# Two reload sets fetched two tiles ahead, and three PSUM tiles that swap banks, in a one-core fp32 layer

## The chip, the cores and the metric

The kernel runs on one core of one Trainium2 chip. The metric is the time of one execution on the device, in microseconds, and the median of several runs is compared. A core has TensorE (PE in the profile, with its weight loads as PEld), VectorE (DVE), ScalarE (ACT), GpSimd (POOL) and SyncE (SP), which here issues nearly all DMAs. Each engine works through its own instructions in the order in which the program put them; an instruction that waits holds everything behind it on that engine. That holds for SP's DMA issues too.

## What is computed

One layer of a decoder trunk for 1024 tokens of 2048 features, all in fp32:

```python
h = rmsnorm(x, g_pre)
u = h @ w_in                       # columns: gq gk gv g_gate g_lr | sq sk sv s_gate
log_a = log_sigmoid(g_lr @ w_a2 + b_a) / 16
o_gla = rmsnorm(gla_chunked(gq, gk, gv, log_a), g_gla_head) * silu(g_gate)   # 4 heads
o_sb  = stick_breaking(sq, sk, sv) * silu(s_gate)                            # 8 heads of 128
mix = concat(o_gla, o_sb) @ w_out
x = x + rmsnorm(mix, g_post)
gate = sigmoid(x @ w_ple_gate + b_ple_gate)
out = x + gate * (p @ w_ple_proj)
```

## The kernel before

Every fp32 operand of a large product is split into a high part, rounded by ScalarE (`hi`, `ah`, `wh`), and a low part, the rest, subtracted by VectorE (`lo`, `al`, `wl`). A product of two such operands takes three matmuls (line 101): high by high, low weight by high activation, high weight by low activation. The tokens are handled in two halves of 512 columns, `hf` 0 and 1.

The input projection goes by units of 128 columns of `w_in`. The first two units run beside the loading of x and fill all four PSUM buffers of the tag `dn` (`first`, evacuated by ScalarE in line 736). From the third unit on `dense` is called: it takes two PSUM tiles of the tag `dn`, and its weights come through `wload`: a DMA into one of two `raw` buffers, a split into one of four `hi` and `lo` buffers each. PSUM has eight banks: four `dn`, two `z`, one `t`, one `o`. The small work of the two attention parts uses `z`, `t` and `o`.

After the second unit two jobs per half are queued as urgent: `norm_first` (the sum of squares of x over all features through a matmul with ones in `rsqrt_mean`, then 1/sqrt of the mean as `rstd`) and `low_rank` (the forget gate's 16 columns, through a matmul with a selection matrix; `W3` steps pass between its split and its matmuls). The evacuation of the third unit and of all later ones multiplies by `rstd`, and the heads' jobs (`gla`, then `sb`) start when no urgent job is left. The jobs are generators; `step()`, called within the dense products, advances one or more of them. `beside` is a third queue of background jobs, of which one piece is taken every `pace[1]` steps. A scheduler then orders the instructions of each engine by its own estimates.

After the last unit comes C11: the eight products of one quarter of the gate weights `w_gate[0, 0]` (`keep_u1`), then eight with `w_gate[1, 0]` (`keep_11`, the last four after the attention's buffers were given back). Beside them the last head's attention ends, and `x_set` brings back two sums of x that were stored to DRAM earlier: the set `S2` beside the first eight products, the set `S1` beside the next four. A set has eight tiles of 128 by 512: each is loaded by a DMA into a buffer of the tag `u` (twelve buffers, shared with the attention) and split into `ah` and `al`. What is not done when the fourth of the `keep_11` products ends is done in a loop without products.

Then the gate stage starts. Its loop over j loads three quarters of the gate weights (`wr`, four buffers of 512 KB, line 880), subtracts twice on VectorE (line 876), splits the results into `wh` and `wl`, and runs two products with `S2` and `S1`. The `wr` buffers lie where the attention's buffers were. A loop that the text calls T4 follows, with the sum of one quarter and a stored difference as weights.

## Time and profile before

| | |
|---|---|
| time, median of 3 runs | 2092.18 us (2090.54 to 2094.57) |
| the profiled execution: its own time | 2090.99 us |
| the profiled execution: its span, first to last instruction | 2089.3 us |
| granted clock of TensorE, mean, as a share of full speed | 0.997 |
| TensorE busy | 2068.5 us, 99% of the span, 9712 matmuls |
| VectorE busy | 1483.5 us, 71% |
| ScalarE busy | 875.1 us, 42% |
| DMA, mean over the span | 169 GB/s |

A matmul of 512 columns is listed with a duration of about 0.39 us, but consecutive ones start about 0.23 us apart: they overlap, and their listed ends are modelled. So the pace of TensorE is read from the starts, and a wait as a start that comes late. The share of 99% is one of overlapping durations; time in which TensorE runs at half its clock counts as busy.

### The profile page before, as it was taken

To read this page: it belongs to the slowest core of one execution; us is meant where nothing else is said; L and a number is where in the kernel's file an instruction comes from. 1 tells how busy PE (TensorE), PEld (TensorE's weight loads), DVE (VectorE), ACT (ScalarE), POOL (GpSimd) and SP (SyncE) were. 2 spreads that over 40 slices of the span, in tenths; PEclk is the share of its full clock that TensorE was granted. 3 is DMA by queue.
4 is the path that set the end of the run, shared out by engine and by line. 5 is a ranking of instruction groups with operands and counts; after the bars stand their busy time and mean duration, and the time that the engine had idled before them with its cause. 6 is when DMAs were issued, how large, how long until landed. Compare 5 with 4: busy or idle time off the path is not lost.

```text
span 2089.3 us, 26740 instructions
## 1 busy us (share of the span) xinstructions
PE 2068.5 (99%) x9712; PEld 1709.3 (82%) x9712; DVE 1483.5 (71%) x2243; ACT 875.1 (42%) x1390; POOL 108.1 (5%) x229
## 2 busy tenths in 40 slices
PE   9999999999999999999999899999999999999998
PEld 6788888888888888888888788888788888788887
DVE  8657777676776676666567667788777687886765
ACT  7333334333464455555456413344233434323332
POOL 4100000000011111101101000000000000000000
PEclk9999999999999999999999999999999999999999
DMA  6222222232344344433335677988977586886763
GB/s 217 69 71 72 86 73 86 66 86 66 76 112 99 102 108 111 110 94 100 80 89 161 207 291 275 324 302 295 328 282 260 183 321 219 295 279 211 238 206 105
DMA packets 229700, 352.81 MB, mean 169 GB/s; under 512 B 124336, under 2 KB 129344, under 8 KB 229568
## 3 DMA queue, kind: packets, MB, share of 16 engines
q1 hardware_dynamic: 228960, 349.00, 52.7%
q10 hardware_dynamic: 576, 2.10, 0.3%
q8 instruction: 76, 1.25, 0.3%
q14 instruction: 56, 0.46, 0.1%
q0 software_dynamic: 32, 0.01, 0.0%
HBM read 249.85 MB, written 73.92 MB: 155 GB/s over the span
## 4 chain that ended last, share of the span: by engine, by line
PE 73%; DMA 10%; DVE 9%; issue 5%; ACT 2%; SPq 1%; POOL 0%; DVEq 0%; ACTq 0%; POOLq 0%
PE dn L101 63%; PE z L101 5%; DMA E<-X 3%; PE o L101 2%; PE t L101 2%; DVE wl L114 1%; DMA wr<-w_out 1%; DMA u<-S1x_d 1%; DVE X L603 1%; DMA ar<-og_d 1%; DVE lo L114 1%; DVE al L114 1%; DMA h_d<-st 1%; DMA ar<-h_d 1%; DVE rstd L235 0%
## 5 line engine op out<-in xcount | busy, mean ns | idle before, releaser
L101 PE MATMUL dn<-ah,hi 128*128 128x512 f32 x1408 | 562.6, 400 | 2.0 <-ACT u L736 1.6
L101 PE MATMUL dn<-ah,lo 128*128 128x512 f32 x1408 | 550.2, 391 | 0.7 <-DVE lo L114 0.7
L101 PE MATMUL dn<-al,hi 128*128 128x512 f32 x1408 | 550.1, 391 | 0.1
L101 PE MATMUL dn<-ah,wl 128*128 128x512 f32 x1216 | 474.9, 391 | 1.6 <-DVE wl L114 1.5
L101 PE MATMUL dn<-ah,wh 128*128 128x512 f32 x1216 | 474.2, 390 | 1.8 <-ACT wh L113 1.8
L101 PE MATMUL dn<-al,wh 128*128 128x512 f32 x1216 | 474.3, 390 | 0.0
L101 PEld LDWEIGHTS dn<-ah,hi 128*128 128x128 f32 x1408 | 265.4, 188 | 60.2 <-issue 3.6
L101 PEld LDWEIGHTS dn<-al,hi 128*128 128x128 f32 x1408 | 264.6, 188 | 57.8 <-DVE al L252 0.5
L101 PEld LDWEIGHTS dn<-ah,lo 128*128 128x128 f32 x1408 | 265.6, 189 | 49.0 <-DVE lo L114 1.3
L113 ACT ACTIVATE wh<-wr 128x1024 fp32r<-128x1024 f32 x152 | 159.1, 1056 | 307.2 <-DVE wr L876 148.5
L101 PEld LDWEIGHTS dn<-ah,wl 128*128 128x128 f32 x1216 | 228.9, 188 | 50.9 <-DVE wl L114 3.3
L101 PEld LDWEIGHTS dn<-ah,wh 128*128 128x128 f32 x1216 | 229.0, 188 | 49.9 <-ACT wh L113 2.5
L101 PEld LDWEIGHTS dn<-al,wh 128*128 128x128 f32 x1216 | 229.0, 188 | 47.7
L114 DVE TENSOR_TENSOR wl<-wr,wh 128x1024 fp32r<-128x1024 f32 x152 | 184.9, 1217 | 6.3 <-ACT wh L113 6.2
L113 ACT ACTIVATE hi<-raw 128x512 fp32r<-128x512 f32 x192 | 119.8, 626 | 147.7 <-PE dn L101 138.5
L114 DVE TENSOR_TENSOR lo<-raw,hi 128x512 fp32r<-128x512 f32 x192 | 135.3, 706 | 52.4 <-ACT hi L113 52.1
L333 ACT ACTIVATE X<-E 128x256 uint16<-128x256 uint16 (+2 forms) x96 | 81.0, 844 | 139.2 <-DMA E<-X 72.0
L876 DVE TENSOR_TENSOR wr<-wr,wr 128x1024 f32<-128x1024 f32 x48 | 58.7, 1224 | 72.0 <-issue 20.0
L603 DVE TENSOR_TENSOR_SCAN X<-X 128x128 f32<-128x128 f32 (+2 forms) x96 | 97.9, 1020 | 14.5 <-POOL X L597 13.1
L618 DVE COPY v<-E 128x512 uint16<-128x512 uint16 (+1 forms) x160 | 64.5, 430 | 48.4 <-DMA E<-X 45.2
L114 DVE TENSOR_TENSOR s<-v,s 128x512 fp32r<-128x512 f32 (+1 forms) x82 | 52.6, 641 | 63.2 <-ACT s L113 62.8
L873 DVE TENSOR_TENSOR wr<-wr,wr 128x1024 f32<-128x1024 f32 x48 | 58.7, 1224 | 43.8 <-DMA wr<-w_g 26.5
(246 smaller groups left out, 2288.7 us busy)
## 6 DMA issues: line engine op xcount, KB each, us to landing
raw<-w_in SPq DMA_DIRECT2D x160, 256.0 KB, 2.7
wr<-w_g SPq DMA_DIRECT2D x64, 512.0 KB, 4.3
wr<-w_out SPq DMA_DIRECT2D x56, 512.0 KB, 4.9
wr<-w_gate SPq DMA_DIRECT2D x40, 512.0 KB, 5.6
g_d<-wr SPq DMA_DIRECT2D x32, 512.0 KB, 2.6
wr<-g_d SPq DMA_DIRECT2D x32, 512.0 KB, 5.1
ar<-h_d SPq DMA_DIRECT2D x28, 512.0 KB, 5.2
ar<-og_d SPq DMA_DIRECT2D x25, 512.0 KB, 5.4
```

Of the source, the lines that this page charges most:

```text
L101: PE.matmul(o, lhsT, rhs, start=start, stop=stop)
L113: A.activation(hi, src, AF.Copy)
L114: (eng or V).tensor_tensor(lo, src, f(hi), op=ALU.subtract)
L333: A.activation(pl.rearrange("p (two n) -> p two n", two=2), src.bitcast(U16)[:, :2 * n].rearrange("p (n two) -> p two n", two=2), AF.Copy)
L603: V.tensor_tensor_scan(rev, rev, rev, initial=kq[:, n:n + 1], op0=ALU.mult, op1=ALU.bypass)
L618: V.tensor_copy(to[:, :, :m, j], w[:, :, 2 * g:2 * g + m])
L873: V.tensor_tensor(dst, a, b, op=ALU.add)
L876: V.tensor_tensor(dst, a, b, op=ALU.subtract)
```

## The change

Four things are edited.

1. The third unit (`u == 2`) accumulates in two `z` banks, not `dn`; the two sums of `norm_first` (`rsqrt_mean` called from there) go to `dn`, not `z`.
2. `W3` is 9, not 4: `low_rank` lets nine steps pass, not four, between its split and its matmuls.
3. `x_set` loads two tiles before its first pause, and then in each piece splits the tile loaded longest ago and loads the one two further on. Before, a piece loaded one tile, and the next piece split it.
4. For the set `S1` a background piece is taken every 2 steps, not every 4 (`pace[1] = 2`).

```diff
-W3 = 4
+W3 = 9
...
-    def dense(wsrc, acts, halves, evac):
-        out_ps = {hf: ps("dn") for hf in halves}
+    def dense(wsrc, acts, halves, evac, bank="dn"):
+        out_ps = {hf: ps(bank) for hf in halves}
...
-    def rsqrt_mean(acc, n, dst, new):
-        z = ps("z")
+    def rsqrt_mean(acc, n, dst, new, bank="z"):
+        z = ps(bank)
...
-            rsqrt_mean(acc[hf], D, acc[hf], lambda dt=F32: at(next(tags), dt=dt))
+            rsqrt_mean(acc[hf], D, acc[hf], lambda dt=F32: at(next(tags), dt=dt), "dn")
...
-                dense(U(u), x_act, HALVES, ev)
+                dense(U(u), x_act, HALVES, ev, "z" if u == 2 else "dn")
...
         def x_set(name, hf):
-            for k in range(8):
+            def load(k):
                 t = at("u")
                 dma2(t, part(sx_d[name][k // 2], k))
-                yield 1
+                return t
+
+            ahead_2 = [load(0), load(1)]
+            yield 1
+            for k in range(8):
                 if k % 2 == 0:
                     wides = act_wide(hf, k // 2)
                 pair = tuple(part(x, k) for x in wides)
-                split(*pair, t)
+                split(*pair, ahead_2.pop(0))
                 g_sets[name].append(pair)
+                if k + 2 < 8:
+                    ahead_2.append(load(k + 2))
+                yield 1
...
         beside.append(x_set("S1", 0))
+        pace[1] = 2
```

Three places show what this does to the order. The first is on TensorE, where the third unit starts. Before (names with numbers: `dn_727` and `dn_728` are the unit's two halves):

```order
L268 MATMUL o_80<-xraw_590,lr_w 32x512
L101 MATMUL dn_727<-ah_123,hi_730 128x512
L101 MATMUL dn_727<-ah_123,lo_731 128x512
L101 MATMUL dn_727<-al_124,hi_730 128x512
L101 MATMUL dn_728<-ah_135,hi_730 128x512
```

And now:

```order
L268 MATMUL o_80<-xraw_590,lr_w 32x512
L101 MATMUL z_727<-ah_123,hi_730 128x512
L101 MATMUL z_727<-ah_123,lo_731 128x512
L101 MATMUL z_727<-al_124,hi_730 128x512
L101 MATMUL z_728<-ah_135,hi_730 128x512
```

The order is the same, the banks are others. Where that unit ends, VectorE had this order (`v<-t` and `v<-o` are the first step of `low_rank` for the two halves, `v<-dn_727` is the third unit's evacuation):

```order
L677 TENSOR_TENSOR v_845<-t_79,rstd_259 128x512
L114 TENSOR_TENSOR s_847<-v_845,s_846 128x512
L677 TENSOR_TENSOR v_886<-o_80,rstd_271 128x512
L685 TENSOR_TENSOR lr_690<-z_881,lr_690 32x512
L114 TENSOR_TENSOR s_888<-v_886,s_887 128x512
L323 TENSOR_TENSOR v_904<-dn_727,rstd_259 128x512
```

And now:

```order
L677 TENSOR_TENSOR v_845<-t_79,rstd_259 128x512
L114 TENSOR_TENSOR s_847<-v_845,s_846 128x512
L323 TENSOR_TENSOR v_893<-z_727,rstd_259 128x512
L323 TENSOR_TENSOR v_896<-z_728,rstd_271 128x512
L685 TENSOR_TENSOR lr_690<-z_925,lr_690 32x512
```

Both evacuations moved ahead of `low_rank`'s result for the first half, and its second half moved behind them. On TensorE the first half's selection matmuls stand 19 matmuls into the fourth unit, where they stood 13 into it, and the heads' first gate matmul (`z<-lr,a2c`) stands 24 dense matmuls later. From the third head's gla work on, TensorE's order is the same again as before.

The second place is ScalarE in C11, where the last head's attention and the set S1 meet. Before:

```order
L333 ACTIVATE X_2345_11059<-E_2344_11053 128x1024
L113 ACTIVATE s_11078<-v_11075 128x512
L113 ACTIVATE ah_11205<-u_11137 128x512
L113 ACTIVATE hi_11240<-raw_11239 128x512
L113 ACTIVATE s_11115<-v_11112 128x384
L113 ACTIVATE ah_11205<-u_11209 128x512
```

And now:

```order
L333 ACTIVATE X_2346_11061<-E_2345_11055 128x1024
L113 ACTIVATE s_11078<-v_11075 128x512
L113 ACTIVATE ah_11141<-u_11106 128x512
L113 ACTIVATE ah_11141<-u_11108 128x512
L113 ACTIVATE hi_11256<-raw_11255 128x512
L113 ACTIVATE s_11119<-v_11116 128x384
```

Two tiles of S1 are split where one was. The last split of S2 (`ah_11069<-u_11073`) stood 10 rows ahead of `s_11078` and now stands 46 rows ahead of it. The last split of S1 had two splits of `raw` weights behind it before the next stage, and now has six.

The third place is SP's queue at the end of C11. Before:

```order
L763 DMA u_11338<-S1x_d_706 128x512
L763 DMA u_11344<-S1x_d_706 128x512
L130 DMA raw_11473<-w_gate 128x512
L130 DMA raw_11491<-w_gate 128x512
L880 DMA wr_11596<-w_gate 128x1024
L880 DMA wr_11598<-w_gate 128x1024
L880 DMA wr_11600<-w_gate 128x1024
L880 DMA wr_11667<-w_gate 128x1024
```

And now (line 888 is the former line 880):

```order
L130 DMA raw_11451<-w_gate 128x512
L888 DMA wr_11596<-w_gate 128x1024
L130 DMA raw_11473<-w_gate 128x512
L888 DMA wr_11598<-w_gate 128x1024
L130 DMA raw_11491<-w_gate 128x512
L888 DMA wr_11600<-w_gate 128x1024
L888 DMA wr_11667<-w_gate 128x1024
```

The loads of S1 are done ahead of this piece, and the first two of the next stage's four loads moved ahead of the last `raw` loads of C11.

## Rows read from the trace of the kernel before

**Rows 1.** The page, busy time of each engine (us, share, instructions)

```profile
PE 2068.5 (99%) x9712; PEld 1709.3 (82%) x9712; DVE 1483.5 (71%) x2243; ACT 875.1 (42%) x1390; POOL 108.1 (5%) x229
```

**Rows 2.** Timeline of TensorE: start, duration, line, tiles, count [idle before <-releaser]

```profile
57.72 1.07 PE L268 MATMUL t<-xraw,lr_w 128*32 128x512 f32 x8
58.71 0.50 PE L101 MATMUL dn<-ah,hi 128*128 128x512 f32 x1
...
60.30 1.07 PE L268 MATMUL o<-xraw,lr_w 128*32 128x512 f32 x8
62.94 0.50 PE L101 MATMUL dn<-ah,hi 128*128 128x512 f32 x1 [1.57 <-ACT u L736]
```

**Rows 3.** Busy time by stretch: PE, PEld, DVE, ACT, POOL (count), PEclk, DMA share, GB/s

```profile
60.00:64.00 4.00, 2.43 (x15) 1.05 (x14) 1.39 (x2) 2.87 (x6) 0.00 (x0) 1.00 0.47 128
1150.00:1165.00 15.00, 12.21 (x50) 8.80 (x49) 9.46 (x16) 8.20 (x14) 0.00 (x0) 0.89 0.69 157
...
1197.00:1210.00 13.00, 10.40 (x32) 7.76 (x31) 9.98 (x10) 3.60 (x4) 0.00 (x0) 0.74 0.72 258
1285.00:1335.00 50.00, 50.00 (x222) 41.23 (x221) 40.68 (x40) 22.34 (x22) 0.00 (x0) 1.00 0.91 317
```

**Rows 4.** Chain of work, first units: start us, us, what

```profile
77.81 11.11 PE dn L101 x49
...
92.67 7.50 PE dn L101 x33
```

**Rows 5.** Timeline of VectorE after the third unit

```profile
88.77 0.69 DVE L114 TENSOR_TENSOR s<-v,s 128x512 fp32r<-128x512 f32 x1 [0.70 <-ACT s L113]
...
92.12 0.69 DVE L323 TENSOR_TENSOR v<-dn,rstd 128x512 f32<-128x512 f32 x1
```

**Rows 6.** Timeline of TensorE, middle of C11

```profile
1154.64 0.50 PE L101 MATMUL dn<-ah,lo 128*128 128x512 f32 x1 [0.48 <-DVE lo L114]
...
1157.55 0.50 PE L101 MATMUL t<-s,u 128*128 128x256 f32 x2 [1.48 <-ACT s L113]
...
1161.41 0.63 PE L101 MATMUL dn<-ah,lo 128*128 128x512 f32 x1
...
1163.75 1.26 PE L101 MATMUL t<-s,u 128*128 128x256 f32 x6 [0.40 <-ACT s L113]
```

**Rows 7.** Timeline of ScalarE in C11

```profile
1148.65 0.63 ACT L113 ACTIVATE ah<-u 128x512 fp32r<-128x512 f32 x1 [3.25 <-DMA u<-S2x_d]
...
1156.88 0.61 ACT L113 ACTIVATE s<-v 128x512 fp32r<-128x512 f32 x1
1159.96 0.63 ACT L113 ACTIVATE ah<-u 128x512 fp32r<-128x512 f32 x1 [2.47 <-DMA u<-S1x_d]
...
1183.03 0.63 ACT L113 ACTIVATE ah<-u 128x512 fp32r<-128x512 f32 x1 [5.18 <-DMA u<-S1x_d]
```

**Rows 8.** Chain of work, end of C11

```profile
1154.40 5.54 DMA u<-S1x_d
...
1166.70 3.19 DMA u<-S1x_d
...
1188.38 8.78 DMA wr<-w_gate
```

**Rows 9.** Timeline of SyncE's DMA queue, end of C11

```profile
1185.02 2.37 SPq L130 DMA_DIRECT2D raw<-w_gate  x2
1187.45 2.12 SPq L880 DMA_DIRECT2D wr<-w_gate  x4
```

**Rows 10.** Timeline of TensorE, first product of the next stage

```profile
1199.69 0.50 PE L101 MATMUL dn<-ah,wh 128*128 128x512 f32 x1 [1.84 <-ACT wh L113]
1200.95 0.79 PE L101 MATMUL dn<-ah,wl 128*128 128x512 f32 x1 [0.76 <-DVE wl L114]
```

**Rows 11.** Timeline of VectorE, last weights of the gate T4 loop

```profile
1327.78 1.22 DVE L114 TENSOR_TENSOR wl<-wr,wh 128x1024 fp32r<-128x1024 f32 x1
```

**Rows 12.** Timeline of TensorE there, the matmul that reads them

```profile
1329.09 0.46 PE L101 MATMUL dn<-ah,wl 128*128 128x512 f32 x1
```

## The prediction

> **What bounds the kernel.** TensorE is busy 99% of the span [rows 1], so only time in which it waits or runs at half its clock can be won. I read first the page's busy times, then busy time by stretch where TensorE's own timeline has late starts, then at each late start the engine named as releaser and what held that. At their normal pace 33 dense matmuls take 7.50 us, 0.227 each [rows 4]. The change touches three stretches with late starts, and each is priced by its rows.
>
> (a) The third unit starts at 62.94 after 1.57 us of idle time that ScalarE's evacuation of the first units ends [rows 2]. From the group of small matmuls before it to this start pass 2.64 us (60.30 to 62.94); one group earlier it was 0.99 (57.72 to 58.71). So 1.65 us are lost. The clock stays at 1.00 [rows 3].
>
> (b) In the middle of C11 the matmuls wait for `lo` (0.48), twice for the attention's `s` (1.48 and 0.40), and then dense ones last 0.63 in place of 0.39 [rows 2, 6]. In 1150 to 1165 TensorE is busy 12.21 of 15 us: 2.79 idle. A granted clock of 0.89 there means that 2 x 0.11 x 15 = 3.3 us ran at 1.2 of 2.4 GHz, and half of that is lost: 1.65. Together 4.4 [rows 3].
>
> (c) The gate stage's first matmul starts at 1199.69 after 1.84 us of idle time for `wh`, the second after 0.76 for `wl` [rows 10]. In 1197 to 1210: 13 - 10.40 = 2.60 idle, and 2 x 0.26 x 13 = 6.8 us at half clock, 3.4 lost: 6.0 [rows 3].
>
> The sum within reach is 1.65 + 4.4 + 6.0 = 12.05 us.
>
> **The change part by part.** *Third unit in `z`.* The two `z` banks are idle there, so the first product no longer waits for ScalarE's evacuations. What is late next is its weights: those of the first two quarters were split before this unit, the two that ScalarE splits just ahead of the evacuations belong to the last two quarters, twelve dense matmuls per half and more away. I take all 1.65; the bounds are 1.0 (a later link shows up) and 1.65. No instruction is added.
>
> *Norm's sums in `dn`.* Their place among the dense matmuls is the same (54 in), the banks they take were emptied some 10 us earlier. Nothing, either way.
>
> *`low_rank` five steps later.* Its first matmul now needs a `z` bank that the third unit filled, so the unit's evacuation must come first, and the order has it next behind `low_rank`'s own split. Before, that split ended at 88.77 + 0.69 = 89.46 [rows 5], when TensorE came to its matmul at 77.81 + 11.11 = 88.92 [rows 4]. Now the bank is free one evacuation of 0.69 [rows 5] later, at 90.2, and TensorE comes six dense matmuls later, at 88.92 + 6 x 0.227 = 90.3; both move 1.65 earlier. So it fits with 0.1 to spare: I take 0, and 0.5 as the upper bound. The first head's gate matmul comes 24 dense matmuls (5.4 us) later, which delays the first heads' side work; from the third head on TensorE's order is the old one, so nothing reaches the attention. For the new interleaving between I take 0, with one wait like the 0.48 of `lo` [rows 6] as a bound on either side.
>
> *S2 two tiles ahead.* The last split of S2 waits 3.25 us for its load, with all of ScalarE's queue behind it: the attention's sigmoids, the `raw` splits, the `s` for which TensorE then waits [rows 7]. Now this split stands 36 rows earlier, beside a load that was issued two tiles before. So ScalarE gets on about 3 us sooner, though each attention tile then still passes through one transposing DMA and one buffer after another; I take 2.4 us for the `s` at 1156.88. The 0.48 wait for `lo` goes, since its split is 2 us earlier too. That brings TensorE to the first `s` at about 1155 (1157.55 less both waits and some 0.6 by which starts around them were late) and `s`, 0.61 long, to 1154.5 to 1155.1, its low part 0.7 later: some 0.5 us of idle time remain.
>
> *S1 two tiles ahead, at twice the pace.* Behind that first `s` ScalarE now splits two tiles of S1 before the next `raw` and the next `s`. On SP the two loads stand among transposes and `raw` loads, so the first starts about 2.4 earlier than the 1154.40 of before [rows 8], at 1152.0, and the second, three issues on, at about 1153.4: not much before they are used. A load of S1 took from 3.19 to 5.54 us [rows 8]. With 5.54 the second lands at 1158.9, two splits and the `s` follow (about 0.5 each, and 0.6 for the low part), and `s` is complete at about 1160.7; TensorE, after six attention and twelve dense matmuls, comes there at about 1159.4. So I take 1.3 us of idle time there; with 3.19 it is none. Behind it, each next pair is issued at least four `raw` splits before ScalarE needs it, and ScalarE's later waits of up to 5.18 us for S1 [rows 7] go; they held nothing that TensorE waited for. Of (b) that leaves 4.4 - 0.5 - 1.3 = 2.6 gained, if the clock doesn't fall. The bounds are 4.4 and 1.0 (the same 1.8 of idle time, and half-clock time of 1.65 as before).
>
> The Trainium skill ("DMA: Bandwidth & Descriptors", section "Anatomy of one DMA") fits a load on the gpsimd path as 2.0 us plus its bytes at 436 GB/s; for the 256 KB of one tile my estimate from it is 2.6 us. These loads go over SP, and the rows give 3.19 to 5.54, so the measurement decides. By the page's price no wait would be left in (b), and the whole sum would be 12.05.
>
> *The gate stage's first weights.* SP issues their four loads behind the last two `raw` loads, at 1187.45 [rows 9], 10 us before C11 ends, and the four take 8.78 us together [rows 8], then come subtractions and splits. In the new order the first goes three `raw` loads before the end, the second two before, the last two behind the final `raw`. A `raw` tile feeds twelve matmuls, 2.7 us, and no split of S1 is between them now, so SP gets through earlier as well. Even if the last two start where all four did, two of four loads are left: by half of 8.78, an estimate, they land 4.4 us sooner, more than the 2.60 of idle time. So the wait goes, and with it the fall of the clock: 6.0, bounds 3 and 6.0. Four loads beside `raw` traffic share the DMA engines; a `raw` that lands late by 2 us still has four split tiles, 10.9 us of work, ahead of it.
>
> *Sum.* 1.65 + 2.6 + 6.0 = 10.25 off the profiled execution's 2090.99 gives 2080.7. Its time is 1.2 below the median of the runs, so as a median: 2092.18 - 10.25 = **2081.9**.
>
> **The rivals.** *The clock falls again.* If what is left to wait in (b) costs half-clock time as before, 1.65 is not won: 2083.6. For it: the same stretch fell after 1.48. Against it: (a) waited 1.57 and kept 1.00 [rows 2, 3]. The Trainium skill ("TensorE: Matmul & The Clock Gate", section "Part 1") states that throttled is the default and activity lifts it, which would let any wait cost twice; the trace shows both cases.
>
> *The weights' loads become the bound.* In 1285 to 1335 the DMA engines are at 0.91 [rows 3], and the split of the last T4 weights ends at 1327.78 + 1.22 = 1329.00, 0.09 us before the matmul that reads it starts [rows 11, 12]. If the chain of loads and splits does not get earlier along with TensorE, what is won in (c) is paid back here. The gain is then 1.65 + 2.6, 2087.9. Against it: the chain's first loads move earlier by as much as TensorE, by the new order rather more.
>
> *Slower.* One mechanism: S1's pairs hold ScalarE. Each of four pairs can wait a whole load (5.54) and then split twice (1.3), with C11's `raw` splits behind it. TensorE has at most four split tiles in stock, 10.9 us; if the stock is down to 4 us, each pair idles it by some 3 us and costs half-clock time of 1.65. Four times 4.6 is 18.6, less 8 won elsewhere: 2102.7. It decides where the stock falls below about 7 us at every pair. Against it: before, ScalarE waited 5.18 for one S1 tile [rows 7] and TensorE ran through.
>
> *Nothing happens*: what bounds (b) is the attention's latency and (c) waits for something else than SP's order; then 1.65 at most, 2090.5.
>
> **How the numbers follow.** About 0.2% (4.2 us) is what a measurement here can tell from no change. Sum as above or better, 2080 to 2083: 0.57. Clock falls, 2083 to 2086: 0.23. Loads the bound, about 2088: 0.11, half of it within 0.2%. Nothing: 0.05. Slower: 0.04. The range reaches from all of 12.05 plus 2 us of spread between runs, 2078, to just short of the loads' case, 2087.5. Faster 0.86, same 0.10, slower 0.04.
>
> **What would show it.** Right: the third unit starts at about 61.3; ScalarE has no wait for S2 near 1148; the first gate `wh` matmul follows C11's last without a gap and the clock there stays at 1.00; about 1.8 us idle in the middle of C11. Wrong: a new wait of low-rank's `z` matmul, a wait for `wl` in T4 that took over the gain, or idle time at every pair of S1.

## The result and the profile after

The changed kernel is **slower**: 2097.65 us in the median of 7 runs, beside 2090.54 for the kernel before in its 7; the ratio is 1.0032 with a 95% interval of 1.0020 to 1.0045. The forecast was 2081.9. Its profiled execution took 2094.28 us (span 2092.6), 3.3 more than that of before. Single executions of one kernel scatter: those of before went from 2085.24 to 2096.02 in the 35 runs beside one set of experiments. So ratios are compared below, and 0.001 of a ratio (2.1 us) is about half the width of their intervals.

The page's line of busy times (after: us, share of the span, instructions) looks as before [rows 1], so it does not show where:

```profile
PE 2068.2 (99%) x9712; PEld 1708.0 (82%) x9712; DVE 1479.1 (71%) x2243; ACT 874.0 (42%) x1390; POOL 108.3 (5%) x229
```

To find the place, take the start of the n-th matmul in the trace of after, minus the start of the n-th in that of before. This offset is -1.7 us at 122 us, -1.9 at 180, +4.5 at 1094, +6.5 at the end of C11, +0.4 at 1217, +3.8 at 1343 and +3.3 at the end. So there is a gain at the start, a loss of 6.4 in the first heads' gla work, a loss of 2 in C11, a gain of 6 at the gate stage's start, and a loss of 3.4 in the loops behind it. Busy time by stretch shows the same places; first after, its columns as in [rows 3]:

```profile
60.00:64.00 4.00, 4.00 (x21) 2.33 (x20) 2.16 (x5) 1.70 (x4) 0.00 (x0) 1.00 0.48 118
180.00:225.00 45.00, 42.84 (x221) 35.03 (x220) 35.82 (x75) 18.39 (x29) 1.61 (x1) 1.00 0.31 84
290.00:345.00 55.00, 52.94 (x274) 43.47 (x274) 39.59 (x83) 21.42 (x36) 1.82 (x2) 1.00 0.39 88
1150.00:1176.00 26.00, 21.57 (x91) 17.17 (x90) 18.41 (x33) 13.72 (x24) 0.00 (x0) 0.87 0.70 200
1197.00:1210.00 13.00, 13.00 (x59) 10.77 (x58) 9.52 (x10) 3.24 (x4) 0.00 (x0) 1.00 0.83 303
1285.00:1346.00 61.00, 59.32 (x255) 47.16 (x255) 48.79 (x49) 25.63 (x25) 0.00 (x0) 1.00 0.88 307
```

and the kernel before, for those stretches that [rows 3] does not have:

```profile
180.00:225.00 45.00, 44.86 (x246) 37.89 (x245) 34.82 (x73) 16.50 (x28) 2.13 (x2) 1.00 0.31 82
290.00:345.00 55.00, 54.88 (x287) 45.78 (x287) 41.39 (x83) 22.05 (x38) 2.13 (x2) 1.00 0.29 77
1150.00:1176.00 26.00, 23.21 (x104) 18.10 (x103) 16.62 (x28) 12.17 (x21) 0.00 (x0) 0.93 0.64 167
1285.00:1346.00 61.00, 61.00 (x271) 50.33 (x270) 48.30 (x49) 25.91 (x26) 0.00 (x0) 1.00 0.90 316
```

TensorE is idle 2.16 us of 45 and 2.06 of 55 where it was idle 0.14 and 0.12. The edits that were meant for 60 to 64 and 1197 to 1210 did what they were meant to do there: no idle time and a clock of 1.00 in both, where [rows 3] has 2.43 busy of 4, and a clock of 0.74.

**The start.** Timeline of TensorE, the third unit (after; compare [rows 2]):

```profile
60.60 1.06 PE L268 MATMUL o<-xraw,lr_w 128*32 128x512 f32 x8
61.59 0.50 PE L101 MATMUL z<-ah,hi 128*128 128x512 f32 x1
```

0.99 us lie between the two starts, as between the same pair one group earlier, and the 1.57 of waiting is gone. Then, in the gla work, new waits (after; each row's last part is the idle time and what ended it):

```profile
191.54 0.63 PE L492 MATMUL t<-c,E 128*128 128x128 f32 x4 [0.57 <-DVE E L390]
200.07 0.68 PE L101 MATMUL z<-X 128*64 128x64 f32 x8 [1.07 <-DVE X L411]
...
305.86 0.50 PE L101 MATMUL z<-E,ones_r 128*128 128x512 f32 x1 [0.68 <-DVE E L114]
313.75 0.86 PE L101 MATMUL z<-X 128*96 128x64 f32 x8 [1.10 <-DVE X L411]
```

What held X at 200 stands in VectorE's timeline (after):

```profile
195.72 0.75 DVE L344 COPY u<-E 128x1024 uint16<-128x1024 uint16 x1 [0.93 <-DMA E<-X]
...
198.63 0.74 DVE L344 COPY u<-E 128x1024 uint16<-128x1024 uint16 x1 [1.37 <-DMA E<-X]
199.26 0.41 DVE L410 TENSOR_TENSOR X<-E,u 128x256 f32<-128x256 f32 x1
199.59 0.42 DVE L411 TENSOR_TENSOR X<-E,u 128x256 f32<-128x256 f32 x1
```

The copy of line 344 is the last step of a later unit's transposed evacuation and waits for a transposing DMA. It has got in front of the head's own X. Before, the same steps of the head stood ahead of that copy, and the copy did not wait:

```profile
191.44 0.42 DVE L410 TENSOR_TENSOR X<-E,u 128x256 f32<-128x256 f32 x1
191.78 0.41 DVE L411 TENSOR_TENSOR X<-E,u 128x256 f32<-128x256 f32 x1
192.12 0.74 DVE L344 COPY u<-E 128x1024 uint16<-128x1024 uint16 x1
```

The wait at 313.75 comes about in the same way: a copy of line 344 that waited 1.15 for its DMA stands at 310.42, ahead of that head's steps. From 180 to 345 these copies wait 6.8 us in all, where they waited 2.2 before and 2.9 in the kernel e2 below. The two waits for X are 2.2 of TensorE's 5.0 us of waits there; behind the others stand other steps of VectorE, and those were not followed to one cause.

**C11.** Timeline of TensorE (after; compare [rows 6]):

```profile
1160.12 0.50 PE L101 MATMUL t<-s,u 128*128 128x256 f32 x2 [1.13 <-ACT s L113]
...
1166.53 0.51 PE L101 MATMUL t<-s,u 128*128 128x256 f32 x2 [2.20 <-ACT s L113]
1167.91 1.11 PE L101 MATMUL t<-s,u 128*128 128x256 f32 x4 [0.88 <-DVE s L114]
...
1169.79 0.63 PE L101 MATMUL dn<-al,hi 128*128 128x512 f32 x1
```

The second `s` is late by 2.20 and its low part by another 0.88, and behind that eleven matmuls start 0.43 apart in place of 0.23, at half the clock. ScalarE's timeline says why (after; compare [rows 7]):

```profile
1159.45 0.61 ACT L113 ACTIVATE s<-v 128x512 fp32r<-128x512 f32 x1
1161.70 0.63 ACT L113 ACTIVATE ah<-u 128x512 fp32r<-128x512 f32 x1 [1.64 <-DMA u<-S1x_d]
1164.92 0.63 ACT L113 ACTIVATE ah<-u 128x512 fp32r<-128x512 f32 x1 [2.59 <-DMA u<-S1x_d]
...
1165.97 0.51 ACT L113 ACTIVATE s<-v 128x384 fp32r<-128x384 f32 x1
```

It stands before two tiles of S1 whose loads SyncE could issue only behind a transpose (its queue, after):

```profile
1155.70 1.24 SPq L336 DMA_TRANSPOSE E<-X  x1
1156.99 0.57 SPq L763 DMA_DIRECT2D u<-S1x_d  x1
...
1158.56 1.95 SPq L763 DMA_DIRECT2D u<-S1x_d  x1
```

The view of DMA issues of after has, for seven of these loads between 1140 and 1175 (line, queue, operation, count, KB each, median us from issue to landing):

```profile
u<-S1x_d SPq DMA_DIRECT2D x7, 256.0 KB, 4.7
```

For loads over SyncE's queue the measurement again decides against the estimate of 2.6 us that the prediction drew from the Trainium skill ("DMA: Bandwidth & Descriptors", section "Anatomy of one DMA").

**The gate stage and the loops.** Its first matmuls follow C11's last without a gap (after; compare [rows 10]), 0.22 later:

```profile
1203.91 0.39 PE L101 MATMUL dn<-al,hi 128*128 128x512 f32 x1
1204.13 0.39 PE L101 MATMUL dn<-ah,wh 128*128 128x512 f32 x1
```

But then TensorE waits for `wl`, for the first time at 1287.14 (compare [rows 11, 12], where it was ready in time). The rows show TensorE, then VectorE, then SyncE's queue.

```profile
1287.14 0.50 PE L101 MATMUL dn<-ah,wl 128*128 128x512 f32 x1 [1.02 <-DVE wl L114]
```

```profile
1284.72 1.23 DVE L881 TENSOR_TENSOR wr<-wr,wr 128x1024 f32<-128x1024 f32 x1 [4.84 <-DMA wr<-g_d]
1285.87 1.22 DVE L114 TENSOR_TENSOR wl<-wr,wh 128x1024 fp32r<-128x1024 f32 x1
```

```profile
1277.57 0.33 SPq L1041 DMA_DIRECT2D g_d<-wr  x1
1281.08 0.32 SPq L888 DMA_DIRECT2D wr<-g_d  x1
```

The load at 1281.08 comes 3.5 us after the last store out of a `wr` buffer, lands for the addition at 1284.72, and the low part ends at 1285.87 + 1.22 = 1287.09, 0.05 before the matmul.

### The profile page after: what moved, and what is told of

The parts are those of the page before. It is cut to its first block, busy times and chain, and to the rows that moved or that the text cites. A ratio compares the mean times of both kernels' runs of the same rounds, so it can differ in the third digit from the quotient of the medians.

```text
span 2092.6 us, 26755 instructions
## 1 busy us (share of the span) xinstructions
PE 2068.2 (99%) x9712; PEld 1708.0 (82%) x9712; DVE 1479.1 (71%) x2243; ACT 874.0 (42%) x1390; POOL 108.3 (5%) x229
## 4 chain that ended last, share of the span: by engine, by line
PE 66%; DMA 14%; DVE 11%; issue 6%; ACT 2%; POOL 0%; SPq 0%; DVEq 0%; ACTq 0%; POOLq 0%
PE dn L101 56%; PE z L101 5%; DMA E<-X 3%; PE t L101 2%; PE o L101 2%; DVE wl L114 2%; DMA wr<-w_gate 2%; DMA wr<-w_g 1%; DMA g_d<-wr 1%; DVE wr L881 1%; DVE wr L884 1%; DVE al L114 1%; DVE X L603 1%; DMA ar<-h_d 1%; DMA ar<-c_d 1%
## 5 line engine op out<-in xcount | busy, mean ns | idle before, releaser
L101 PE MATMUL dn<-ah,hi 128*128 128x512 f32 x1376 | 550.0, 400 | 0.8 <-ACT ah L251 0.8
L101 PE MATMUL dn<-ah,lo 128*128 128x512 f32 x1376 | 538.1, 391 | 0.0
L101 PE MATMUL dn<-al,hi 128*128 128x512 f32 x1376 | 537.9, 391 | 0.0
L101 PEld LDWEIGHTS dn<-ah,hi 128*128 128x128 f32 x1376 | 259.7, 189 | 56.7 <-issue 5.3
L101 PEld LDWEIGHTS dn<-al,hi 128*128 128x128 f32 x1376 | 258.9, 188 | 56.2 <-DVE al L252 0.3
L101 PEld LDWEIGHTS dn<-ah,lo 128*128 128x128 f32 x1376 | 259.7, 189 | 46.9
```

The costliest lines, as they stand in the source:

```text
L101: PE.matmul(o, lhsT, rhs, start=start, stop=stop)
```

## The experiments

All but the last two were timed in five rounds against the kernel before. This table has every kernel's ratio, and the offsets (in us) of its profiled execution against the first profile of before: at the start of the matmul that before starts at 1094 (ahead of C11), at C11's last, 60 matmuls into the gate stage (1217), in T4 (1343), at 1778, and at the last. (Where 24 matmuls are left out or added, those behind are counted from the end.)

| kernel | 1094 | C11's last | 1217 | 1343 | 1778 | last | ratio, 95% interval |
|---|---|---|---|---|---|---|---|
| before, a second profile (e18) | -0.9 | -1.4 | -5.9 | -2.4 | -3.6 | -2.9 | |
| after | +4.5 | +6.5 | +0.4 | +3.8 | +3.3 | +3.3 | 1.0032 (1.0020 to 1.0045) |
| after, a second profile (e17) | +3.1 | +0.7 | -5.4 | +3.0 | +2.6 | +3.1 | |
| e1: start edits | +4.1 | +3.8 | +2.2 | +2.1 | +0.2 | +1.7 | 1.0019 (1.0008 to 1.0029) |
| e2: start edits, W3 = 6 | -0.9 | -2.0 | -6.5 | -1.5 | -1.5 | +0.9 | 0.9996 (0.9986 to 1.0007) |
| e13: start edits, W3 = 8 | -1.2 | -1.4 | -5.7 | -3.5 | -2.4 | -2.2 | 1.0000 (0.9990 to 1.0009) |
| e14: start edits, W3 = 10 | +4.2 | +4.5 | -1.4 | +1.4 | +1.5 | +2.7 | 1.0032 (1.0020 to 1.0044) |
| e3: W3 = 9 alone | +6.1 | +8.0 | +2.6 | +5.9 | +4.8 | +4.8 | 1.0036 (1.0023 to 1.0049) |
| e4: C11 edits | -0.6 | -1.4 | -7.1 | -2.4 | -0.7 | 0.0 | 1.0008 (0.9998 to 1.0018) |
| e5: all edits, W3 = 6 | -1.3 | -1.5 | -7.6 | -4.0 | -3.5 | -0.9 | 1.0006 (0.9997 to 1.0016) |
| e9: loads ahead alone | 0.0 | -0.5 | -6.5 | -5.0 | -4.3 | -4.2 | 1.0001 (0.9992 to 1.0010) |
| e10: pace of 2 alone | +0.1 | +1.3 | -4.8 | +0.6 | +2.3 | +2.0 | 1.0029 (1.0020 to 1.0038) |
| e6: e5, S1 still earlier | -1.0 | +1.3 | -4.8 | -0.4 | -2.2 | -1.3 | 1.0014 (1.0003 to 1.0025) |
| e7: e5, less DMA in T4 | -1.7 | -0.8 | -6.8 | -3.4 | -3.7 | -3.0 | 1.0006 (0.9995 to 1.0017) |
| e8: e5, five wr buffers | -1.1 | -0.9 | -7.0 | -7.1 | -7.9 | -1.8 | 1.0008 (0.9996 to 1.0020) |
| e11: e2, five wr buffers | -1.3 | -1.2 | -5.2 | -5.3 | -7.0 | -1.1 | 1.0011 (0.9999 to 1.0022) |
| e12: e2, pace of 2, five wr buffers | -0.1 | -0.1 | -6.2 | -6.3 | -5.8 | -0.8 | 1.0014 (1.0005 to 1.0023) |
| e15: 24 matmuls less | -0.2 | -4.7 | -2.6 | -2.0 | -0.5 | +0.3 | 1.0017 (1.0008 to 1.0026) |
| e16: 24 matmuls more | +0.1 | +5.7 | -0.4 | +5.4 | +7.1 | +7.8 | 1.0045 (1.0033 to 1.0057) |

### Which half loses

e1_start is the change without the C11 edits (`x_set` as before, no `pace[1] = 2`); e4_c11 has those alone.

> Only the edits at the start are made (third unit in z, norm's sums in dn, W3 = 9); C11 is as before. In the profile of the changed kernel TensorE was 1.7 us earlier at 122 us and 4.6 us later at 324 us, against the kernel before. Theory A (the loss between 180 and 324 us belongs to the start edits and is carried to the end): the time is 4.6 us above the kernel before, give or take 1, +0.22%. Rival B (the loss there is an accident of that one execution): 1.7 below, -0.08%. Rival C (runs of the changed kernel were 7 us slower in the median, its profiled one only 3.3, so something varies from run to run, and it is the start): +7 to +9 in the median, with a spread of some 8 us between runs.

> Only the edits in C11 are made (loads two tiles ahead, S1 at pace 2); the start is as before. From the profile of the changed kernel: 1.9 us lost in the middle of C11 (1140 to 1175), 6.0 won at the gate stage's first product, 3.4 paid back to waits for wl at 1287 to 1345: sum -0.7 us, within 0.05% of the kernel before. Rival (my forecast for these edits): -8.6 us, -0.41%. Rival C (what varies from run to run lies here): +2 to +4 us in the median, with a spread of some 8 us.

The start edits cost 0.0019, the C11 edits 0.0008 with an interval that just includes none; the sum of 0.0027 lies within the interval of the whole change. The loss of the start edits is that of theory A: +4.1 at 1094, after -1.4 at 122. The C11 edits give nothing, and my forecast of 8.6 for them is refuted: -7.1 at 1217 has become -2.4 at 1343 and 0.0 at the end.

### The delay of low_rank

e2, e13 and e14 are e1 with another number, e3 is the kernel before with one line changed:

```diff
-W3 = 9
+W3 = 6      # e2_start_w6; 8 in e13_w8, 10 in e14_w10
```

```diff
-W3 = 4
+W3 = 9      # e3_w9, banks as before
```

> Start edits with W3 = 6 in place of 9; C11 as before. The orders of TensorE, ScalarE, VectorE and SyncE then differ from before in the start alone (TensorE's last changed row stands in the fourth unit), and the first heads' work stands where it stood. Theory A (the five steps' delay of low_rank moves the first heads' work to a worse place; the banks are harmless): 1.7 us below the kernel before, -0.08%, and no late starts between 180 and 324 us beyond those of before. Rival B (the z banks lent to the third unit disturb the heads): still +4 to +5 us, +0.2%.

> Only W3 = 9; all banks and C11 as before. Theory A (delay alone makes the loss): 6.3 us above the kernel before, +0.30%, with waits for X and E in 190 to 320 us like those of the changed kernel. Rival B (banks): within 1 us of before.

> Start edits with W3 = 8, C11 as before. The first gate matmul of the heads (lr by a2c) stands 12 matmuls later in TensorE's order than with W3 = 6 or 7, and 12 earlier than with W3 = 9. Theory A (the later the first heads' work, the more of it meets the units' evacuations): about half of the loss between e2_start_w6 and e1_start, ratio 1.0005 to 1.0015, and late starts between 180 and 325 us that cost 1 to 4 us more than in e2. Rival B (the loss starts at one point, with 24 matmuls): ratio as e2_start_w6, 0.9996. Rival C (any delay costs all of it): as e1_start, 1.002.

> As e13_w8 with W3 = 10: the first gate matmul stands 36 matmuls later than with W3 = 6. Theory A: more than e1_start, ratio 1.0025 to 1.004. Rival B (it is the phase against the units that decides): less than e1_start, 0.999 to 1.0015.

W3 = 9 alone loses 0.0036 and 6.1 us by 1094, with the banks as before: the delay makes the loss, not the lent banks. With the banks lent and W3 = 6 the offset stays at -0.9 and no loss is left. With 8 (12 matmuls later than with 6) it is -1.2 and 1.0000, with 9 (24 later) +4.1 and 1.0019, with 10 (36 later) +4.2 and 1.0032. In the times the loss grows with the delay, but it begins between 8 and 9: nothing like the half that theory A expected shows at 8, so rival B describes the beginning better; that is read from the traces, since the interval of the times at 8 reaches 1.0009 and would hold a part of the loss. Between 6 and 9, all else alike, lie 5.0 us in the traces at 1094, and 0.0023 of 2091 = 4.8 us in the times.

So the start edits could have been had without loss, with W3 = 6; with W3 = 4 and the third unit in `z`, `low_rank`'s matmul would need a bank that VectorE frees only behind `low_rank`'s own result (its order before), and the engines would wait for each other in a circle. That is read from the order; the pair wasn't run. Even then the 1.7 us of the start do not show in the time: 0.9996, with an interval that includes 1.

### The C11 edits

e9_ahead has the two-ahead `x_set` at the old pace of 4, e10_pace only `pace[1] = 2`, and e5_w6_c11 the whole change with W3 = 6. e6 adds to e5:

```diff
+        s1_set = x_set("S1", 0)
         for j in range(8):
+            if j == 6:
+                next(s1_set)
             small_product(x_act[0][:8], w_gate[0, 0, j], keep_u1(j))
...
-        beside.append(x_set("S1", 0))
+        beside.append(s1_set)
```

> The whole change with W3 = 6 in place of 9, so that the first heads' work stays where it was. Theory A (the changed kernel loses 6 us to the five steps alone; the rest of it comes out even): 5 to 6 us below the changed kernel, that is 1 to 2 below the kernel before, ratio 0.9993, with TensorE 1.5 us early at 330 us, some 6 to 8 us early at 1199 and 2 to 4 us early at 1345. Rival B (my forecast without the delay): 10 below before, 0.995. Rival C (the delay hid something that is later lost anyway): no better than the changed kernel, 1.003.

> Only the loads two tiles ahead, at the old pace of 4; the start is as before. ScalarE's queue still has two splits of S1 between the first s and the second, as in the changed kernel; SyncE's four first loads of the gate stage stand behind the last raw loads, as before. Theory A (the early loads of S2 and the pair of S1 make the middle of C11, the pace makes the gate stage's start): the middle of C11 (1100 to 1196) loses as much as in e4_c11, 4.9 give or take 1.5, and the gate stage's first weights cost 2 to 6 us as before; ratio 1.000 to 1.002. Rival B (the pace makes the pair's wait): the middle of C11 loses under 3.5.

> Only the pace of 2 for S1, loads as before; the start is as before. SyncE's queue has the first two of the gate stage's loads ahead of the last raw loads, as in the changed kernel; ScalarE's queue has one split of S1 between the first and the second s, and two around the raw split behind it. Theory A: the gate stage's start costs nothing (6 us won), and the middle of C11 loses what it lost before or one wait for S1 more (5.5 to 8); 3 to 4 us are paid back to the waits for wl up to 1345; ratio 0.998 to 1.001. Rival B (the loads ahead are what frees SyncE's queue): the gap at the gate stage's start stays.

> As e5_w6_c11, but the first two loads of S1 are issued beside the seventh product of C11's first eight, some 10 us sooner, ahead of five transposes in SyncE's queue. Theory A (the attention's second s waits because ScalarE stands before it at two splits whose loads were issued too late): ScalarE's two waits for S1 there (1.6 and 2.6 us in the changed kernel) go, and with them TensorE's 2.4 and 0.9 us and the half clock behind them (2.4 us lost): TensorE is 4 to 5.5 us earlier at 1175 than in e5. Of that, theory B (the gate loops' loads set the time from there on) lets nothing reach the end, ratio as in e5; if B is wrong, 4 to 5 us of it do, ratio 0.997. Rival C (the s itself is late through the transposes, not through ScalarE): the waits stay.

e5 is back at the time of before (1.0006), some 5.4 us below after, as theory A wanted. It is not below before, though TensorE was 7.6 us ahead at 1217.

From 1094 to C11's last matmul, executions with both C11 edits (after, e17, e4, e5) change by +1.9, -2.4, -0.8 and -0.2, executions with C11 as before (before, e18, e1, e2, e3, e13, e14) by 0.0, -0.5, -0.3, -1.1, +1.9, -0.2 and +0.3. The means are -0.4 and 0.0: the edits changed where TensorE waits there, but hardly how long in sum, and two executions of one kernel differ by more. Where it changed can be split. Between the matmuls that before starts at 1153 and at 1160, with the first `s` between them, the seven executions with loads two tiles ahead (after, e17, e4, e5, e7, e8, e9) win 1.5 to 2.9 us, and the six others with C11 as before win nothing (they lose 0.1 to 2.1). From there to 1168, with the second `s`, the seven lose 0.3 to 4.2, and the six win 0.4 to 2.0. So the loads ahead did win at the first `s` what they were made for, and the second `s` took it back. The half clock behind the waits differs too: in after's second profile the stretch 1150 to 1176 kept 1.00, at 2.95 us of idle time:

```profile
1150.00:1176.00 26.00, 23.05 (x113) 18.64 (x112) 17.86 (x32) 12.68 (x22) 0.00 (x0) 1.00 0.65 190
```

e6 did not tell what it was to tell. The first two tiles of S1 were split early (at 1147.62 and 1148.66), but then tiles three and four stood in front of the second `s`, with loads issued as late as the first two's had been. ScalarE's rows in e6:

```profile
1159.76 0.63 ACT L113 ACTIVATE ah<-u 128x512 fp32r<-128x512 f32 x1 [0.98 <-DMA u<-S1x_d]
1162.64 0.63 ACT L113 ACTIVATE ah<-u 128x512 fp32r<-128x512 f32 x1 [2.25 <-DMA u<-S1x_d]
...
1163.69 0.51 ACT L113 ACTIVATE s<-v 128x384 fp32r<-128x384 f32 x1
```

The wait moved to the next pair, and TensorE lost 3.5 us at the attention's matmuls near 1132 and 1143. So that a pair of loads holds ScalarE is what the rows show, but no run took the loads' wait away.

With the loads ahead alone (e9) there was no gap at the gate stage's start either, though SyncE's four loads stand behind the last `raw` loads there: what I expected of e9 on that point was wrong. With the pace alone (e10) the gap went too, but the time is 1.0029. That is worse than both together, and its profiled execution (+2.0, the second shortest of its 11 runs) shows only a part of it; the rest stays open.

### What becomes of time won ahead of the loops

e15 and e16 shift TensorE's arrival at the gate stage by a known amount: the term high weight by low activation of the last three products of C11 is left out, or done twice.

```diff
-                    mm(p, hi[:, sl], al, False, k == 7)
+                    for i in range(terms):      # 0 in e15, 2 in e16, in three of the sixteen products
+                        mm(p, hi[:, sl], al, False, k == 7 and i == terms - 1)
```

> The kernel before, but in the last three of C11's products the term high weight by low activation is left out: 24 matmuls, 24 x 0.227 = 5.45 us of TensorE's work less, right ahead of the gate stage. Nothing else is left out. Theory A (the weights of the gate loops set the time from there to 1345, TensorE waits for them if it comes earlier): at 1345 TensorE is 0 to 2 us earlier than before, and the time is 0 to 2 us less, ratio 0.999 to 1.000. Rival B (TensorE's work sets the time): 5.45 less, ratio 0.9974.

> The kernel before with the same 24 matmuls done twice in the last three of C11's products: 5.45 us more of TensorE's work ahead of the gate stage (that term counts double in the result). Theory A (before, weights and TensorE meet about even): the gate stage's first wait goes, the time is 1 to 4 us more, ratio 1.0005 to 1.002. Rival B (TensorE's work sets the time): 5.45 more, ratio 1.0026. Rival C (the loads have no slack and move along with C11's end, since they wait for buffers that C11 frees): 5.45 more too, with the first wait still there; e15_less tells B from C.

With 5.45 us of work **less**, TensorE reaches the gate stage 4.7 us earlier and waits there for the first weights (e15, TensorE):

```profile
1192.78 0.39 PE L101 MATMUL dn<-ah,lo 128*128 128x512 f32 x1
1197.60 0.80 PE L101 MATMUL dn<-ah,wh 128*128 128x512 f32 x1 [4.44 <-ACT wh L113]
```

At the end it is 0.3 later than before, and the time is 1.0017, above what either theory expected. With 5.45 us **more**, the gap at the gate stage goes (-0.4 at 1217: all of the added work fits into it), and then it comes back as waits for `wl`: +5.4 at 1343. Its 1.0045 is above all three expectations; another 2.4 us of it are lost behind 1343, and why is open. The view of groups of instructions from 1205 to 1346 (busy, mean ns of one, idle before and what ended it), for before, e16 and e8 in turn:

```profile
L101 PE MATMUL dn<-ah,wl 128*128 128x512 f32 x206 | 80.7, 392 | 0.0
```

```profile
L101 PE MATMUL dn<-ah,wl 128*128 128x512 f32 x199 | 78.7, 395 | 2.8 <-DVE wl L114 2.6
```

```profile
L101 PE MATMUL dn<-ah,wl 128*128 128x512 f32 x208 | 81.0, 389 | 0.0
```

So a gap ahead of the loops and waits within them stand for one another. I read it thus: while TensorE stands in the gap, the loads build up a stock. It fits that e1, whose gap cost 4.5 us, loses nothing from 1217 to 1343, and that no four-buffer execution without a gap is free of the loss: after, e17, e4 and e5 lose 3.4, 8.4, 4.7 and 3.6 us there, and the least is the 1.6 of e9. (Of e17's 8.4, 4.5 stand at one wait of 2.57 us at 1252.10 and at the half clock behind it.) From 1094 to 1343, these four executions with the C11 edits change by -1.4 us in the mean, and the seven with C11 as before by -1.3. The edits moved the waiting from one place to another.

e7 and e8 ask what bounds the loads there; e11 and e12 put the fifth buffer on e2, and on e2 with the pace.

```diff
-                finish(staged(c11_d[i]), 0, i)
+                c = staged(c11_d[i])
+                finish(c, 0, i, c)      # e7_no_o: no load of o
```

```diff
-            raw = mt("wr", 4)
+            raw = mt("wr", 5)      # e8_wr5, e11_w6_wr5, e12_best
```

> As e5_w6_c11, but beside T4 four loads of 512 KB are left out: the gated sums of the first half's first eight feature tiles are multiplied by themselves, not by the attention's output o. Theory A (in T4 the DMA engines' throughput bounds the weights): the waits for wl between 1280 and 1345 (3 to 4.5 us in the changed kernel and in e4_c11) fall under 1.5, TensorE at 1345 is 2 to 3 us earlier than in e5, and about as much of it reaches the end unless the next stages take it back. Rival B (the ring of load, addition, split and store bounds them, not throughput): waits as in e5, time within 1 us of e5.

> As e5_w6_c11, but with five wr buffers in place of four, so one more load of the gate loops can be under way or in stock. Theory B of e7 (the ring bounds the weights): the waits for wl at 1280 to 1345 go, and so do those near 1490, 1720 and 1900; 3 to 6 us below e5, ratio 0.997. Theory A (throughput): waits as in e5, the time within 1.5 us of it. Rival C: loads that start earlier crowd the raw loads at C11's end or other stages' loads and cost 2 to 4 us.

> The start edits with W3 = 6 and five wr buffers, C11 as before. In e8_wr5 the fifth buffer took the waits for wl at 1267 to 1345 away; TensorE was 8 us ahead of before at 1780 and then lost 4 us twice at the ph products near 1800 and 1980. Theory A (from 1350 on the later stages have a slack that runs out again and again: what comes early waits there): 2089 to 2091, ratio 0.998 to 1.0005. Rival B (those two losses were an accident of one execution): 3 to 5 us below before, ratio 0.9975.

> What the runs so far speak for, together: the start edits with W3 = 6 (1.5 us), the pace of 2 with the old loads (the gate stage's start, up to 6), five wr buffers (no payback in T4, 3 to 4). By the sum TensorE is 7 to 9 us ahead of the kernel before at 1345. Theory A (later stages take back what comes early, as in e8_wr5): the time is 0 to 4 us below before, ratio 0.998 to 1.000. Rival B: 7 us below, ratio 0.9965.

With 2 MB less of loads beside T4 (e7 leaves four loads of `o` out) the waits stay: 3.5 us are lost from 1217 to 1343, in e5 3.6, while the DMA engines' busy share from 1285 to 1346 falls from 0.92 to 0.85. That alone proves less than I expected, for 1.8 of the 3.5 are lost by 1295, and e5 issues the first load of `o` at 1296.89; behind 1295 it is 1.7 against 2.7. With a fifth buffer the waits are gone in all three kernels: nothing is lost from 1217 to 1343 (from -7.0 to -7.1, -5.2 to -5.3 and -6.2 to -6.3), and the DMA engines move more there, 302 to 308 GB/s where e5 has 283. So their throughput is not the bound. Busy time by stretch in e8:

```profile
1285.00:1346.00 61.00, 61.00 (x271) 50.54 (x270) 44.48 (x45) 22.76 (x22) 0.00 (x0) 1.00 0.82 303
```

So the ring of four buffers (load, addition, split, store) is the bound; that SyncE issues loads in another order with five belongs to this, and was not told apart. But the 6 to 8 us that TensorE is then ahead at 1778 are lost behind it, to the products with `ph` (e8, TensorE):

```profile
1799.91 0.50 PE L101 MATMUL z<-ph,pl 128*128 128x512 f32 x1 [2.90 <-DVE pl L114]
...
1981.09 0.50 PE L101 MATMUL t<-ph,pl 128*128 128x512 f32 x1 [1.47 <-DVE pl L114]
```

e11 and e12 have the waits near 1980 too (1.14 and 2.07; 0.36 and 2.08), and before has none from 1940 to 2000, so they were no accident of one execution. The clock falls behind them as well: in e11 TensorE goes from 7.5 ahead at 1975 to 1.1 ahead at 1990, with 3.2 us of idle time and a mean clock of 0.89. Whether coming early makes them, or the order of those stages, which a fifth buffer changes as well, was not tried. No kernel of the study is faster than before by more than its uncertainty; the lowest ratio is that of e2, 0.9996. e8 was expected at 0.997 and came out at 1.0008, and e12, for which even the cautious theory had 0.998 to 1.000, at 1.0014.

### Two more profiles

> The changed kernel once more, for a second profile. Theory A: up to 1100 us TensorE's late starts are the same within 1 us as in the first profile (W3's loss is in the order); what differs lies in C11 and the loops behind it, by up to 5 us. Rival B: the loss at 180 to 325 us itself varies by more than 2 us.

> The kernel before once more. In e2_start_w6 and e11_w6_wr5, whose C11 has the order of before, the gate stage's first weights cost 1.4 to 2 us of late starts and no half clock, in the profile of before 6. Theory A (this stall differs from one execution to the next): 1 to 4 us here, with waits for wl up to 1345 where it is small. Rival B (the 6 us belong to the kernel before): 5 to 7 us.

The loss of the gla work repeats: +3.1 at 1094 after -1.8 at 180 in the second execution of after. What differs is C11 and behind (+6.5 and +0.7 at C11's last), as theory A had it. In the second execution of before, the wait at the gate stage is 0.30 in place of 1.84, then the same 0.76, and the clock does not fall (e18, TensorE):

```profile
1196.03 0.39 PE L101 MATMUL dn<-al,hi 128*128 128x512 f32 x1
1196.71 0.50 PE L101 MATMUL dn<-ah,wh 128*128 128x512 f32 x1 [0.30 <-ACT wh L113]
1197.98 0.50 PE L101 MATMUL dn<-ah,wl 128*128 128x512 f32 x1 [0.76 <-DVE wl L114]
```

It is 4.4 us cheaper than in the first, and 3.5 of that go to waits for `wl` by 1343. The two profiled executions of after took 2094.28 and 2094.12 us, the two of before 2090.99 and 2088.11: the means are 4.6 apart, of 6.7 (0.0032 of 2091) in the ratio. Where the longer executions of after (up to 2100.48) lose the rest stays open.

## Why the prediction was wrong, point by point

- **Third unit in `z`** (1.65 forecast): right. The wait went, the unit starts at 61.59 (61.3 was named), and TensorE is 1.7 ahead at 122. That low_rank's `z` matmul would just fit was right too: no wait stands there. Norm's sums in `dn` were never run alone.
- **`low_rank` five steps later** (0 forecast, 0.5 as the upper bound): **this step failed, and it is why the change is slower and not even.** The prediction saw that the first heads' work comes 24 matmuls later, noted that the order is the old one from the third head on, and took 0 for the interleaving between, "with one wait like the 0.48". It was 5.0 us in the traces (e1 against e2), 4.8 in the times. That TensorE's order is restored later only says that no more is lost there; between, VectorE's order had put a unit's copy, which waits for a DMA, ahead of the head's own steps, twice within 3 us near 200 and again near 310. Those waits for X are 2.2 us of 5.0; that W3 makes the whole loss is shown by e3 and by e1 against e2, and what holds each of the other waits is not. That VectorE's order differs over this stretch could be read beforehand; I priced it without reading the rows.
- **S2 ahead** (2.4 sooner at the first `s`): right in kind, a little less in size. ScalarE has no split of S2 and no wait for one near the first `s` any more. TensorE was 4.1 later there than before, so the `s` at 1159.45 is 1155.4 on the clock of before, 1.5 sooner than 1156.88; it still holds TensorE for 1.13, not 0.5. Seven executions win 1.5 to 2.9 at this place.
- **S1 ahead, at twice the pace** (1.3 of idle time at the second `s`): mis-sized. It was 2.20 + 0.88, and the rival that the clock falls came true in that execution. On the clock of before, the first load's issue at 1156.99 is 1152.9, 0.9 behind the forecast (1152.0), and the second's at 1158.56 is 1154.5 (1153.4). That issue took 1.95, and the split began 6.36 us behind its start, at 1164.92 or 1160.8, where I had the load take 5.54 at most and land at 1158.9. Of the 2.6 us won in C11, the means over executions leave 0.4, which is less than two executions of one kernel differ by.
- **The gate stage's first weights** (6.0): the gap went, but the price was wrong and the mechanism is not shown. Every execution with the whole of the C11 edits runs through with at most 0.4 us lost there. But so does e9, where the four loads stand behind the last `raw` loads as before, and so does e14, whose C11 is that of before; so the new place of the loads need not be what closed the gap. And 6.0 was what the gap cost in one execution. Over seven with C11 as before, TensorE makes up 3.7 us on that execution between C11's last matmul and 1217, in the mean; so the gap costs 6.0 - 3.7 = 2.3 on average, and in e14 nothing.
- **The rival "the weights' loads become the bound"** (0.11): this is what happened, in every four-buffer execution without a gap (1.6 to 8.4 us from 1217 to 1343, where (c) is worth 2.3 on average). Its counter-argument, that the chain's loads move earlier with TensorE, overlooked that the chain is a ring: its first loads may start earlier, but its pace is that of buffers coming free. e15 shows how wrong the frame of the sum was: 5.45 us of TensorE's own work taken away there gave nothing.
- **The rival "slower"** (0.04) named S1's pairs at every one of four places; one pair cost time, and the slowdown came from elsewhere.

As measured in the traces, the terms are: 1.7 won and 4.9 to 6.4 lost at the start, and about 0 from C11 on, with two more microseconds in the median that no profile explains. In the times, 16.9 us lie between the 10.25 forecast as won and the 6.7 lost (0.0032). The step of `low_rank` is 4.8 of them, and it makes the half of the change whose loss is clear of the noise (e1). The C11 edits, forecast to win 8.6 and measured in e4 at 0.0008, or 1.7 lost with an interval that includes none, are 10.3: the larger part of the miss. The rest is the start's 1.65, of which e2 shows 0.8, and about 1 that no run accounts for.

## What to carry to other kernels

Where a change delays a chain that runs beside a main loop, read the new order of the engine that serves both (here VectorE) row by row until it is the old one again: here the loss was the sum over several waits, not one. Before a stall is priced, ask for a second execution, and ask what follows it: ahead of a loop whose weights pass through a ring of buffers, a gap may be stock for later, and here removing it gave nothing while the ring stayed at four buffers. Even then a later stage that waits for its own weights may take the gain back, as the products with `ph` did here.

## What was not expected of the hardware

Two executions of one program, with one order on each engine, differed by 4.4 us at a single place (3.49 and 1.95 us from C11's last matmul to the second of the gate stage, and the half clock behind it in one of them), and by 5.8 us at C11's last matmul (after and e17). In e17 idle times of 1.13 and 0.88 us before the second `s` left the clock at 1.00; in after, 2.20 and 0.88 at the same place were followed by matmuls at half of it. Taking work off the busiest engine made the program slower (e15, 1.0017), and adding 5.45 us of it cost 1.0045, some 9 us.
